# A hybrid HGRN2 + mLSTM layer on one core: finished token tiles are evacuated behind the next weight split, and the steps from w_out to the FFN stand in another order

## The chip, the core and the metric

The kernel runs on one core of a Trainium2 chip. The time is that of one execution on the device, in microseconds (us). A core has a matrix engine (TensorE, PE in the profile; PEld are its weight loads), a vector engine (VectorE, DVE), an activation engine (ScalarE, ACT), a general engine (GpSimd, POOL) and an engine that here only issues transfers (SyncE, SP). Each engine runs its own instructions in the order in which they were issued and waits for others through semaphores. Matrix products are added up in PSUM, from where DVE or ACT must fetch ("evacuate") them.

## The reference

One layer works on 128 context tokens and 256 sample tokens of width D = 2048. Shift, scale and gate come from the conditioning vector. Cut to what matters here, with `rms_norm(x, g) = x * rsqrt(mean(x*x) + EPS) * g`:

```python
h = rms_norm(x, g_pre_mix) * (1.0 + sc_a) + sh_a
y, new_st = mixer(h, ...)        # h @ w_in, HGRN2 and mLSTM scans, w_up, gates, then @ w_out
x = x + gt_a * rms_norm(y, g_post_mix)
h = rms_norm(x, g_pre_ffn) * (1.0 + sc_f) + sh_f
a, b = jnp.split(h @ w_ffn_in, 2, axis=-1)          # D_FF = 5632 each
x = x + gt_f * rms_norm((jax.nn.silu(a) * b) @ w_ffn_out, g_post_ffn)
```

The outputs are x for both groups of tokens and the final scan states of the context tokens.

## The kernel before

All weight matrices are cut into blocks of 128 x 128 and streamed from HBM in the order of use, 16 blocks to a load (`raw`, 3 buffers) and 8 blocks to a *piece*. Products of 32-bit numbers are made of three products of shorter ones: a piece is split by ACT into a high half (`high`, L951, tile `wh`, instruction at L362) and by DVE into the rest (`low`, L962, tile `wl`, L966). Both have 3 buffers; five pieces around the change have buffers of their own (`xwh`, `xwl`). The activations are split in the same way. For each block TensorE then runs high x high, high x low and low x high.

`run_piece` (L1018) is the step of the main loop: it issues the load two units ahead, the `low` of piece i+1, some extra work, the `high` of piece i+2, and then the products of piece i. For most matrices `products` keeps the weights as the stationary operand and 384 tokens as columns (L984 to L986). For w_out and w_ffn_out `products_t` (L994) keeps 128 tokens as the stationary operand and 512 output columns of the weights as the moving one (L1009 to L1011): 18 matmuls to a piece, 6 for each of three token tiles t. A *block end* is the place where the three accumulators of 512 output columns n are finished; `products_t` then calls `evac_t` (L1079) at once.

- For w_out, `evac_out` (L1341) squares the accumulator on ACT (L1315), multiplies it on DVE by the post-norm gain into `yg` (L1344), squares that on ACT and multiplies it by `x1` on DVE with a running sum (L1346). There are 4 blocks of 8 pieces. Of the last block the last 6 pieces are run token by token: token 0 of all six, then token 1, then token 2.
- After a token's last column `norms` (L1353) makes both norm factors from the sums. `x1_part(t, n)` (L1363) forms the new x in 512 columns (DVE, L1365) and its normed copy in `yg` (ACT, L362). `h2_transpose` (L1370) turns four squares of `yg` on TensorE (L1373), and `h2_part` (L1375) applies scale and shift on ACT (L364, tile `h`) and splits into `hi` (DVE, L1383) and `lo` (L1384), the moving operand of the FFN.
- The first three FFN pieces (the head) need only column quarter n = 0. They are run on tokens 0 and 1 first (256 columns), then on token 2 (128 columns). The pieces after them need quarter 1, and so on; each of the next six pieces carries the transposes of one more token tile.
- For w_ffn_out the inner dimension is cut into six groups. Each adds its part to `yacc` in SBUF (L1087). In the last group, `end_tile` (L1506) follows: ACT squares `yacc` (L1315), DVE multiplies by the post-norm gain (L1513); at the last 512 columns it makes the norm factor, adds x in four instructions (L1521) and stores. The last 3 pieces are again run token by token.

The order of all this is that of the program text from w_out on; the planner `schedule` places only the work of the scans and of the late modulation.

## Time and profile before

| | |
|---|---|
| median of 3 runs | 2432.37 us (2429.99 to 2435.18) |
| profiled execution, its own time | 2430.1 us |
| span of its instructions | 2428.3 us |
| PE busy | 2359.6 us (97%) |
| PEld busy | 2210.5 us (91%) |
| DVE busy | 1466.4 us (60%) |
| ACT busy | 931.0 us (38%) |
| mean granted clock | 0.988 |

Busy time is the sum of an engine's instructions; matmuls overlap in the pipeline, so PE's is no measure of its speed. A granted clock of 1.00 is 2.4 GHz, 0.50 is 1.2 GHz. In a list of waits a row names the engine and instruction that waited, behind `<-` the engine and instruction that released it, and then the total, the number of waits and the longest, in us. In a timeline the first number is the start from the beginning of the span, the second the duration; a bracket at the end is the idle time of the engine just before and what ended it. w_out runs from about 1129 to 1275 us, the last group of w_ffn_out from about 2350 us to the end.

### The profile page before, as it was taken

How to read it: one execution, taken by the hardware profiler on the slowest of the kernel's cores; microseconds unless marked ns; L12 is line 12 of the kernel's file. 1: busy time of each engine (PE TensorE's matmuls, PEld its weight loads, DVE VectorE, ACT ScalarE, POOL GpSimd, SP SyncE). 2: the span in 40 equal slices, each digit the busy share in tenths (PEclk: the TensorE clock that was granted, in tenths of full speed). 3: DMA queues.
4: the chain of work that ended last, by engine and by line, in shares of the span. 5: the costliest groups of instructions: out<-in, count | busy, mean ns of one | idle time of the engine just before them, and what ended most of it. 6: DMA issues, size and time to landing. Idle time of an engine off the chain costs nothing. (4 is left out here: it accounts for less than half of the span.)

```text
span 2428.3 us, 33115 instructions
## 1 busy us (share of the span) xinstructions
PE 2359.6 (97%) x13519; PEld 2210.5 (91%) x13519; DVE 1466.4 (60%) x2237; ACT 931.0 (38%) x1384; POOL 207.8 (9%) x277
## 2 busy tenths in 40 slices
PE   7999899999999999999998999999999999999996
PEld 5889899999999999999778998999899899899895
DVE  5777788776657889885344788333333433433435
ACT  5335555655444222224445333332233223223232
POOL 1115743420000000000000000000000000000000
PEclk9999999999999999999998999999999999999998
DMA  8863324333325666665322555333333333333341
GB/s 353 310 251 146 111 101 182 151 131 142 121 79 188 244 230 233 235 226 209 120 104 74 213 219 223 122 122 139 121 123 139 117 126 122 125 134 128 117 174 70
DMA packets 70809, 393.05 MB, mean 162 GB/s; under 512 B 8416, under 2 KB 8576, under 8 KB 36736
## 3 DMA queue, kind: packets, MB, share of 16 engines
q1 hardware_dynamic: 68256, 383.54, 42.3%
q0 software_dynamic: 2400, 7.38, 0.9%
q8 instruction: 106, 1.74, 0.3%
q14 instruction: 47, 0.39, 0.0%
HBM read 386.14 MB, written 4.76 MB: 161 GB/s over the span
## 5 line engine op out<-in xcount | busy, mean ns | idle before, releaser
L984 PE MATMUL mm<-hi,wh 128*128 128x384 f32 (+1 forms) x2944 | 998.4, 339 | 5.6 <-ACT wh L362 3.0
L986 PE MATMUL mm<-hi,wl 128*128 128x384 f32 (+1 forms) x2944 | 985.6, 335 | 0.7 <-DVE wl L966 0.7
L985 PE MATMUL mm<-lo,wh 128*128 128x384 f32 (+1 forms) x2944 | 985.0, 335 | 0.0
L362 ACT ACTIVATE wh<-raw 128x1024 fp32r<-128x1024 f32 x515 | 543.0, 1055 | 628.4 <-PE mm L985 355.7
L966 DVE TENSOR_TENSOR wl<-raw,wh 128x1024 fp32r<-128x1024 f32 x515 | 625.4, 1230 | 168.2 <-ACT wh L362 167.9
L984 PEld LDWEIGHTS mm<-hi,wh 128*128 128x128 f32 x2944 | 555.3, 189 | 17.4 <-issue 8.3
L985 PEld LDWEIGHTS mm<-lo,wh 128*128 128x128 f32 x2944 | 555.1, 189 | 1.4
L986 PEld LDWEIGHTS mm<-hi,wl 128*128 128x128 f32 x2944 | 554.7, 188 | 1.2 <-DVE wl L966 1.2
L820 DVE SCALAR_TENSOR_TENSOR acc_acc<-raw_w,st,acc_acc 128x512 f32<-128x512 f32 x480 | 335.0, 754 | 0.0
L1011 PE MATMUL mm<-wl,gh 128*128 128x512 f32 x528 | 210.7, 399 | 8.6 <-DVE wl L966 8.6
L1009 PE MATMUL mm<-wh,gh 128*128 128x512 f32 x528 | 210.8, 399 | 0.0
L1010 PE MATMUL mm<-wh,gl 128*128 128x512 f32 x528 | 210.2, 398 | 0.0
L1069 DVE TENSOR_TENSOR fs<-mm,fs 128x384 f32<-128x384 f32 x44 | 24.5, 558 | 185.5 <-ACT fs L364 185.5
L1011 PEld LDWEIGHTS mm<-wl,gh 128*128 128x128 f32 x528 | 100.2, 190 | 34.1 <-DVE wl L966 9.9
L1074 DVE TENSOR_TENSOR fs<-mm,fs 128x384 f32<-128x384 f32 x44 | 24.5, 557 | 171.5 <-PE mm L986 171.5
L1009 PEld LDWEIGHTS mm<-wh,gh 128*128 128x128 f32 x528 | 100.1, 190 | 24.2 <-issue 0.4
L1010 PEld LDWEIGHTS mm<-wh,gl 128*128 128x128 f32 x528 | 100.2, 190 | 23.9
L1333 POOL DMA_DIRECT2D d_f<-gt_f x1 | 0.5, 518 | 1202.4 <-ACT gt_f L362 1202.4
L1087 DVE TENSOR_TENSOR yacc<-mm,yacc 128x512 f32<-128x512 f32 x60 | 41.4, 691 | 97.9 <-PE mm L1011 97.6
L362 ACT ACTIVATE gh<-fs 128x384 fp32r<-128x384 f32 x44 | 23.1, 525 | 166.3 <-DVE fs L1074 166.3
L984 PE MATMUL mm<-oh,wh 128*128 128x384 f32 x256 | 86.6, 338 | 0.0
L986 PE MATMUL mm<-oh,wl 128*128 128x384 f32 x256 | 85.9, 336 | 0.0
(307 smaller groups left out, 2072.9 us busy)
## 6 DMA issues: line engine op xcount, KB each, us to landing
raw<-ws SPq DMA_DIRECT2D x260, 1024.0 KB, 5.1
raw_w<-wm SPq DMA_DIRECT2D x128, 512.0 KB, 3.3
wm<-wm SPq DMA_DIRECT2D x64, 512.0 KB, 6.2
xs<-xt SPq DMA_DIRECT2D x4, 768.0 KB, 7.5
x<-xk SPq DMA_DIRECT2D x3, 1024.0 KB, 6.8
out_y<-yacc SPq DMA_DIRECT2D x12, 256.0 KB, 2.1
GM<-d_m POOLq DMA_DIRECT2D x2, 1024.0 KB, 11.5
gain<-d_f POOLq DMA_DIRECT2D x8, 256.0 KB, 5.4
```

The lines of the kernel that those rows point to most:

```text
L362: sc.activation(out, in_, func, bias=0.0, scale=scale)
L820: ve.scalar_tensor_tensor(get(acc)[:, c], get(w)[:, i], col, get(acc)[:, c], ALU.mult, ALU.add)
L966: ve.tensor_tensor(lo, src, hi.bitcast(F32), ALU.subtract)
L984: te.matmul(acc, hi[:, s], xh[:, b:e], start=first, stop=False)
L985: te.matmul(acc, hi[:, s], xl[:, b:e], start=False, stop=False)
L986: te.matmul(acc, lo[:, s], xh[:, b:e], start=False, stop=last)
L1009: te.matmul(acc, xh[:, c], hi[:, s], start=first, stop=False)
L1010: te.matmul(acc, xl[:, c], hi[:, s], start=False, stop=False)
L1011: te.matmul(acc, xh[:, c], lo[:, s], start=False, stop=last)
L1069: ve.tensor_tensor(s, acc, s, ALU.mult)
L1074: ve.tensor_tensor(s, acc, s, ALU.mult)
L1087: ve.tensor_tensor(y, acc, y, ALU.add)
```

## The change

`products_t` no longer evacuates a finished accumulator at once: it puts the evacuation on a list `post`, and `flush` issues the list. `run_piece` calls `flush` behind the `low` of the next piece and ahead of everything else. In the last group the products with the post-norm gain go on the same list, so that they come behind the three adds. Where pieces are written out by hand, `flush` is called behind the splits. The sum with `x1` in `evac_out` writes a spare SBUF tile (one of the two buffers of `h`) and no longer the accumulator. Transposes and `h2_part` of a tile become one step `part_u`, issued ahead of the products that it stood beside; the `x1_part` steps and the `high` and `low` of four FFN pieces move, and no computation is added or left out.

```diff
@@ -1011,7 +1011,14 @@
                 te.matmul(acc, xh[:, c], lo[:, s], start=False, stop=last)
                 seen[k] += 1
                 if last:
-                    evac_t(key, t, accs.pop(k))
+                    post.append(lambda key=key, t=t, acc=accs.pop(k): evac_t(key, t, acc))
+
+    post = []
+
+    def flush():
+
+        while post:
+            post.pop(0)()
 
     pos = [0]
 
@@ -1020,6 +1027,7 @@
         if i % 2 == 0:
             load(i // 2 + RAW - 1)
         low(i + 1)
+        flush()
         for o in placed.get(i, ()):
             o.fn()
         for fn in extra:
@@ -1343,7 +1351,8 @@
         square(junk, acc, stats[:, t, 0, n:n + 1])
         ve.tensor_tensor(y, acc, GM[:, CT[t], col(n)], ALU.mult)
         square(junk, y, stats[:, t, 1, n:n + 1])
-        ve.scalar_tensor_tensor(acc, y, 2.0, x1[:, t, col(n)], ALU.mult, ALU.mult,
+        junk2 = fp.tile([P, 512], F32, tag="h2", bufs=2, name="h2")
+        ve.scalar_tensor_tensor(junk2, y, 2.0, x1[:, t, col(n)], ALU.mult, ALU.mult,
                                 accum_out=stats[:, t, 2, n:n + 1])
 
     def x_square(k):
@@ -1407,13 +1416,18 @@
         run_piece(todo)
 
 
+
+    def part_u(t, n):
+        h2_transpose(t, n)
+        h2_part(t, n)
+
     run_piece()
     run_piece([lambda: load((a0 + 4) // 2), lambda: high(a0 + 2)])
-    last = [a0 + k for k in range(TAIL_OUT)]
-    pos[0] = p_ffn
-    high(a0 + 3)
     low(a0 + 1)
     low(a0 + 2)
+    flush()
+    last = [a0 + k for k in range(TAIL_OUT)]
+    high(a0 + 3)
     load(p_ffn // 2)
     high(a0 + 4)
     low(a0 + 3)
@@ -1423,32 +1437,32 @@
     load(p_ffn // 2 + 1)
     for i in last:
         products_t(i, (0,), True)
+    flush()
     norms(0)
     x1_part(0, 0)
+    high(p_ffn)
     x1_part(0, 1)
-    high(p_ffn)
     low(p_ffn)
     load(p_ffn // 2 + 2)
     for i in last:
         if i == last[-1]:
-            h2_transpose(0, 0)
+            part_u(0, 0)
         products_t(i, (1,), True)
+    flush()
     norms(1)
-    h2_part(0, 0)
     x1_part(1, 0)
     for k, i in enumerate(last):
         if i == last[-1]:
-            h2_transpose(1, 0)
+            high(p_ffn + 2)
+            low(p_ffn + 2)
+            part_u(1, 0)
         products_t(i, (2,), False)
-        if k == 1:
+        if k == 0:
             high(p_ffn + 1)
             low(p_ffn + 1)
-        if k == 2:
-            high(p_ffn + 2)
-            low(p_ffn + 2)
     load(p_ffn // 2 + 3)
+    flush()
     norms(2)
-    h2_part(1, 0)
     x1_part(2, 0)
 
 
@@ -1457,35 +1471,28 @@
     cur.clear()
     cur.update(h2)
     head = [p_ffn + k for k in range(HEAD_FFN)]
+    x1_part(1, 1)
     for i in head:
         if i == head[-1]:
-            h2_transpose(2, 0)
+            part_u(2, 0)
         products(i, (0, 2 * P), True)
-    h2_part(2, 0)
     for k, i in enumerate(head):
-        x1_part(k, 1) if k else None
-        if k == 1:
-            h2_transpose(0, 1)
-            h2_part(0, 1)
-        if k == 2:
-            h2_transpose(1, 1)
-            h2_part(1, 1)
-        products(i, (2 * P, T))
+        part_u(k, 1)
         if k == 0:
+            x1_part(2, 1)
             high(p_ffn + 3)
             low(p_ffn + 3)
         if k == 1:
+            x1_part(0, 2)
             high(p_ffn + 4)
-    h2_transpose(2, 1)
-    h2_part(2, 1)
+        products(i, (2 * P, T))
     pos[0] = p_ffn + HEAD_FFN
 
     rest = [(t, n) for n in (2, 3) for t in range(3)]
-    x1_part(*rest[0])
     for k, (t, n) in enumerate(rest):
-        todo = [lambda t=t, n=n: h2_transpose(t, n), lambda t=t, n=n: h2_part(t, n)]
+        todo = [lambda t=t, n=n: part_u(t, n)]
         if k + 1 < len(rest):
-            todo.insert(0, lambda r=rest[k + 1]: x1_part(*r))
+            todo.append(lambda r=rest[k + 1]: x1_part(*r))
         run_piece(todo)
     close_pool("f")
     close_pool("wx")
@@ -1510,16 +1517,16 @@
         y = yacc[0][:, t, col(n)]
         square(junk2[3], y, ysum[:, t, n:n + 1])
         if n < 3:
-            ve.tensor_tensor(y, y, GF[n][:, CT[t]], ALU.mult)
+            post.append(lambda: ve.tensor_tensor(y, y, GF[n][:, CT[t]], ALU.mult))
             return
...
@@ -1536,13 +1543,14 @@
         cur.update(gts if pieces[i][0][3][0] == "fo" else h2)
         run_piece(todo)
     last = [n_pieces - TAIL_FO + k for k in range(TAIL_FO)]
-    pos[0] = n_pieces
     for i in last:
         high(i)
         low(i)
+    flush()
     for t in range(3):
         for i in last:
             products_t(i, (t,), True)
+        flush()
     for name in list(pools)[::-1]:
         close_pool(name)
```

DVE at the first block end in w_out (`wl`: low half of a piece; L1344/L1352 the product with the gain, L1346/L1355 the sum), before:

```order
```order
L1318 TENSOR_TENSOR acol<-acol,vt 128x32
L966 TENSOR_TENSOR wl<-raw,wh 128x1024 x8
L1344 TENSOR_TENSOR yg<-mm,GM 128x512
L1346 SCALAR_TENSOR_TENSOR mm,stats<-yg,x_11124 128x512
L1344 TENSOR_TENSOR yg<-mm,GM 128x512
L1346 SCALAR_TENSOR_TENSOR mm,stats<-yg,x_11124 128x512
L1344 TENSOR_TENSOR yg<-mm,GM 128x512
L1346 SCALAR_TENSOR_TENSOR mm,stats<-yg,x_11124 128x512
L966 TENSOR_TENSOR wl<-raw,wh 128x1024 x8
```

and now:

```order
```order
L1326 TENSOR_TENSOR acol<-acol,vt 128x32
L966 TENSOR_TENSOR wl<-raw,wh 128x1024 x9
L1352 TENSOR_TENSOR yg<-mm,GM 128x512
L1355 SCALAR_TENSOR_TENSOR h_11351,stats<-yg,x_11124 128x512
L1352 TENSOR_TENSOR yg<-mm,GM 128x512
L1355 SCALAR_TENSOR_TENSOR h_11356,stats<-yg,x_11124 128x512
L1352 TENSOR_TENSOR yg<-mm,GM 128x512
L1355 SCALAR_TENSOR_TENSOR h_11361,stats<-yg,x_11124 128x512
L966 TENSOR_TENSOR wl<-raw,wh 128x1024 x8
```

One more split stands ahead of the three token tiles. ACT at the head of the FFN (`h`: scaled and shifted transposes; `yg`: normed x; `wh`, `xwh`: high half of a piece), before, from the end of `norms(2)`:

```order
```order
L364 ACTIVATE tot<-tot,zero 128x1
L364 ACTIVATE h_12016<-tp,mod_110,acol 128x128 x4
L362 ACTIVATE yg<-x_11124,tot 128x512
L364 ACTIVATE h_12108<-tp,mod_110,acol 128x128 x4
L362 ACTIVATE wh<-raw 128x1024
L362 ACTIVATE yg<-x_11124,tot 128x512
L364 ACTIVATE h_12150<-tp,mod_110,acol 128x128 x4
L362 ACTIVATE xwh<-raw 128x1024
L362 ACTIVATE yg<-x_11124,tot 128x512
L364 ACTIVATE h_12191<-tp,mod_110,acol 128x128 x4
L364 ACTIVATE h_12227<-tp,mod_110,acol 128x128 x4
L362 ACTIVATE yg<-x_11124,tot 128x512 x2
```

and now, from the same place:

```order
```order
L364 ACTIVATE tot<-tot,zero 128x1
L362 ACTIVATE yg<-x_11124,tot 128x512 x2
L364 ACTIVATE h_12098<-tp,mod_110,acol 128x128 x4
L364 ACTIVATE h_12134<-tp,mod_110,acol 128x128 x4
L362 ACTIVATE yg<-x_11124,tot 128x512
L362 ACTIVATE wh<-raw 128x1024
L364 ACTIVATE h_12176<-tp,mod_110,acol 128x128 x4
L362 ACTIVATE yg<-x_11124,tot 128x512
L362 ACTIVATE xwh<-raw 128x1024
L364 ACTIVATE h_12217<-tp,mod_110,acol 128x128 x4
L364 ACTIVATE h_12254<-tp,mod_110,acol 128x128 x4
L362 ACTIVATE yg<-x_11124,tot 128x512
```

Before, the first `h` here is that of token 1; it now stands further up, ahead of token 2's squares and norm factors. Each `yg` (the product of an `x1_part`) now follows the `h` of the tile before it, where it stood ahead of it. DVE at the end of the last group (L1087/L1095 the adds, L1513/L1520 the gain products, `tail` the last 512 columns), before:

```order
```order
L966 TENSOR_TENSOR wl<-raw,wh 128x1024 x3
L1087 TENSOR_TENSOR yacc<-mm,yacc 128x512
L1513 TENSOR_TENSOR yacc<-yacc,gain 128x512
L1087 TENSOR_TENSOR yacc<-mm,yacc 128x512
L1513 TENSOR_TENSOR yacc<-yacc,gain 128x512
L1087 TENSOR_TENSOR yacc<-mm,yacc 128x512
L1513 TENSOR_TENSOR yacc<-yacc,gain 128x512
L966 TENSOR_TENSOR wl<-raw,wh 128x1024 x2
L1087 TENSOR_TENSOR yacc<-mm,yacc 128x512
L1515 TENSOR_TENSOR tail<-yacc,gain 128x512
```

and now:

```order
```order
L966 TENSOR_TENSOR wl<-raw,wh 128x1024 x3
L1095 TENSOR_TENSOR yacc<-mm,yacc 128x512 x3
L1520 TENSOR_TENSOR yacc<-yacc,gain 128x512 x3
L966 TENSOR_TENSOR wl<-raw,wh 128x1024 x4
L1095 TENSOR_TENSOR yacc<-mm,yacc 128x512 x3
L1520 TENSOR_TENSOR yacc<-yacc,gain 128x512 x3
L1095 TENSOR_TENSOR yacc<-mm,yacc 128x512
L1522 TENSOR_TENSOR tail<-yacc,gain 128x512
L1524 TENSOR_REDUCE tot<-ysum 128x1
```

The last two splits stand ahead of the third block's evacuation where they stood behind it, and its gain products follow the three adds.

## Rows read from the trace of the kernel before

**Rows 1.** Waits of PE, 1060:1350 and 2340:2430: total, times, longest
```profile
PE mm L1011 <- DVE wl L966: 7.1, 3, 2.4
PE mm L984 <- DVE hi L1383: 6.6, 1, 6.6
PE tp L1373 <- ACT yg L362: 6.3, 2, 4.3
...
PE mm L1011 <- DVE wl L966: 8.6, 3, 4.8
```

**Rows 2.** PE timeline, first and third w_out wait: start, duration
```profile
1168.92 0.50 PE L1011 MATMUL mm<-wl,hi 128*128 128x512 f32 x1 [2.40 <-DVE wl L966]
...
1241.16 0.50 PE L1011 MATMUL mm<-wl,hi 128*128 128x512 f32 x1 [2.34 <-DVE wl L966]
```

**Rows 3.** Windows: length, busy time by engine, PEclk, DMA, GB/s
```profile
1210.00:1230.00 20.00, 20.00 (x90) 16.57 (x89) 6.13 (x5) 4.90 (x5) 0.00 (x0) 1.00 0.36 124
1205.30:1208.50 3.20, 3.20 (x9) 2.44 (x9) 1.22 (x2) 0.00 (x0) 0.00 (x0) 0.51 0.89 333
...
2389.80:2393.00 3.20, 3.20 (x9) 2.52 (x8) 0.98 (x1) 0.00 (x0) 0.00 (x0) 0.52 0.00 0
```

**Rows 4.** ACT and DVE timeline, splits after the three blocks
```profile
1168.59 1.04 ACT L362 ACTIVATE wh<-raw 128x1024 fp32r<-128x1024 f32 x1
...
1203.09 1.99 ACT L362 ACTIVATE wh<-raw 128x1024 fp32r<-128x1024 f32 x2
...
1239.99 1.04 ACT L362 ACTIVATE wh<-raw 128x1024 fp32r<-128x1024 f32 x1
...
1239.88 1.22 DVE L966 TENSOR_TENSOR wl<-raw,wh 128x1024 fp32r<-128x1024 f32 x1
```

**Rows 5.** PE timeline, token 1 of the last block, and transposes (L1373)
```profile
1254.72 0.39 PE L1009 MATMUL mm<-wh,hi 128*128 128x512 f32 x1
...
1290.23 0.60 PE L1373 MATMUL tp<-ct,yg 128*128 128x128 f32 x4
...
1296.24 0.62 PE L1373 MATMUL tp<-ct,yg 128*128 128x128 f32 x4
...
1299.33 0.62 PE L1373 MATMUL tp<-ct,yg 128*128 128x128 f32 x4
...
1327.38 0.60 PE L1373 MATMUL tp<-ct,yg 128*128 128x128 f32 x4
...
1331.98 0.60 PE L1373 MATMUL tp<-ct,yg 128*128 128x128 f32 x4
```

**Rows 6.** Timeline, token 0 of the last block; two groups by line
```profile
1254.98 0.69 ACT L1315 ACTIVATE junk<-mm,zero 128x512 f32<-128x512 f32 x1 [7.02 <-PE mm L1011]
...
1255.80 0.69 DVE L1344 TENSOR_TENSOR yg<-mm,GM 128x512 f32<-128x512 f32 x1 [6.39 <-ACT junk L1315]
...
1259.77 1.34 ACT L362 ACTIVATE yg<-x,tot 128x512 f32<-128x512 f32 x2
...
L1365 DVE SCALAR_TENSOR_TENSOR x<-yg,tot,x 128x512 f32<-128x512 f32 x12 | 8.9, 745 | 0.0
L1346 DVE SCALAR_TENSOR_TENSOR mm<-yg,x 128x512 f32<-128x512 f32 x12 | 8.4, 700 | 0.4
```

**Rows 7.** ACT and DVE timeline, one unit in the order h, lo, yg
```profile
1279.84 1.49 ACT L364 ACTIVATE h<-tp,mod,acol 128x128 f32<-128x128 f32 x4
...
1281.82 0.69 DVE L1384 TENSOR_TENSOR lo<-h,hi 128x512 fp32r<-128x512 f32 x1
...
1283.27 0.72 ACT L362 ACTIVATE yg<-x,tot 128x512 f32<-128x512 f32 x1 [1.94 <-DVE x L1365]
```

**Rows 8.** DVE timeline, the end of the last group
```profile
2396.93 0.69 DVE L1087 TENSOR_TENSOR yacc<-mm,yacc 128x512 f32<-128x512 f32 x1 [6.15 <-PE mm L1011]
...
2409.59 0.69 DVE L1087 TENSOR_TENSOR yacc<-mm,yacc 128x512 f32<-128x512 f32 x1 [3.59 <-PE mm L1011]
...
2419.80 0.68 DVE L1087 TENSOR_TENSOR yacc<-mm,yacc 128x512 f32<-128x512 f32 x1
```

More of the change, by code (lines that the diff above doesn't have):

```diff
@@ L1518, in end_tile @@
         rstd1(r, s, D)
-        for n in (3, 0, 1, 2):
-            y, o = yacc[0][:, t, col(n)], junk2[t] if n == 3 else yacc[0][:, t, col(n)]
-            ve.scalar_tensor_tensor(y, o, r, x1[:, t, col(n)], ALU.mult, ALU.add)
-            sy.dma_start(out_y[:, t, col(n)], y)
+        for m in (3, 0, 1, 2):
+            y, o = yacc[0][:, t, col(m)], junk2[t] if m == 3 else yacc[0][:, t, col(m)]
+            ve.scalar_tensor_tensor(y, o, r, x1[:, t, col(m)], ALU.mult, ALU.add)
+            sy.dma_start(out_y[:, t, col(m)], y)
     last_fb = last_piece["fb", KF - 1]
```

## The prediction

> **What bounds the kernel now.** I read the page first: TensorE is busy 97% of the 2428.3 us span and no other engine passes 60%, so time is won only where TensorE stands still, or where work follows its last matmul. Next I read its list of waits, cut to the two stretches that the change touches [rows 1]: w_out and the start of the FFN, and the last FFN output group. The reader is to see few, long waits: 20.0 us in the first stretch, 8.6 in the second. Third, the timeline of TensorE at those waits [rows 2, 5]: in w_out it waits each time for a `wl`, the low half of the weight split, in the second piece after a block of 512 output columns is finished. Fourth, what DVE and ACT do then [rows 4, 6]: DVE is still multiplying, squaring and adding the three finished token tiles, and the `wl` stands behind that in its queue. Last, the granted clock [rows 3]: after the second w_out wait it is 0.51 for 3.2 us, so TensorE is near 1.2 GHz instead of 2.4; the same follows other waits.
>
> A matmul of 512 columns takes (20 + 0.39)/90 = 0.227 us from start to start at full clock [rows 3], so a piece of 18 takes 4.08, and one token's 6 of a piece 1.36.
>
> **A. The three block ends in w_out.** Now the split of piece i+1 stands ahead of the evacuation of piece i-1. The first wait is 2.40 us idle after a matmul of 0.39, 2.79 from start to start, so 2.56 lost; the third loses 2.51 [rows 2]. What is late next: the `wh` behind the squares on ACT, and its `wl`. At the first end that `wh` starts at 1168.59 [rows 4], takes 1.04, and its `wl` 1.22 more, so that is there at 1170.9. TensorE wants it 18 matmuls after 1168.92 - 2.56, at 1170.4: 0.5 is waited, 2.1 won. At the other two no square of `x` stands before the `wh`, which comes 0.7 earlier: nothing is waited. These win 2.56 and 2.51, and 1.6 each for the stretch at half clock that then has no cause (half of 3.2). At the third the split must also feed six pieces at token pace: `wh` at 1239.99 gives `wl` by 1242.3, then one every 1.2 against 1.36 wanted. **A = 2.1 + 4.2 + 4.1 = 10.4.** The squared product with `x1` now writes a spare SBUF tile instead of PSUM: 12 instructions of 0.70, and the nearest row that goes from SBUF to SBUF is 0.745 [rows 6]. On the path it stands three times, so between 0.7 x 3 = 2.1 worse and 2.1 better; I take the near row, 0.1, as nothing.
>
> **B. From w_out into the FFN.** Before, from the square of token 0 at 1254.98 [rows 6] to the last transposes at 1331.98 [rows 5] pass 77.0 us. TensorE's own work in it: two tokens of 8.16 and transposes of 0.36 (17.0); three pieces of 256 columns and three of 128 with four transposes (6.01 from 1290.23 to 1296.24 is one of each and a transpose, 3.09 to 1299.33 is a small piece with its transpose, so 2.92, 2.71 and 0.38: 18.4); five units of 4.60 (1327.38 to 1331.98); less 0.26 by which the square starts after token 1's first matmul, 1254.72: 58.2. So 18.8 is lost now, 12.9 of it in the waits [rows 1], the rest at half clock.
>
> After, I follow the queues as printed. The parts: square to `yg` is 4.79, of which 3.97 from the product with GM [rows 6]; `h` to the end of `lo` is 1281.82 + 0.69 - 1279.84 = 2.67 and `h` to `yg` 3.43 [rows 7], in just the order h, hi, lo, x1, yg that now stands everywhere; a `wh` holds ACT for 0.95 (two take 1.99 [rows 4]).
> - Let token 1 be finished at time 0. The `h` of token 0 ends at 0.35 and its `lo` holds DVE to 1.57; then the product, `yg` at 5.54, two `wh` as before, and `h` of token 1 at 8.04, now ahead of token 2's squares and norm factors where it stood behind them; its `lo` is ready at 10.7. TensorE comes to the first FFN piece at 8.16 + 0.36 = 8.5: 2.1 waited, where 6.6 was.
> - Count now from 8.5. Token 2: square 0.9, product 2.1, `yg` 6.1; its transposes are due at 7.9, no wait. `h`, hi and lo are done at 11.2, when the 128-column pieces want them.
> - Those pieces go at 3.09 each, but x1_part now stands behind part_u in both queues, so that a unit runs h, hi, lo, x1, yg, wh in one chain: 3.43 + 0.62 + 0.95 = 5.0 (0.62 is what a `yg` holds ACT for, 1.34 for two less 0.72). Three units from 11.2: TensorE is at the first 384-column piece at 20.9, the `lo` of (2,1) at 24.5: 3.7 waited, where 4.3 was and the half clock behind it.
> - The last five units want 4.60 and get 5.0; the first has slack, the others wait 0.3 to 0.4, 1.4 in all.
>
> 2.1 + 3.7 + 1.4 = 7.2. Two of the waits are of the length after which the clock fell before; each such stretch costs up to 1.6, none costs nothing, and of 3.2 for both I take 2.2. **B = 18.8 - 7.2 - 2.2 = 9.4**, with 7.2 to 11.6 from the clock alone.
>
> **C. The last FFN group.** Two block ends: 8.6 - 4.8 = 3.8 idle [rows 1], plus 0.16 each as above, 4.1, and one stretch at half clock (0.52 for 3.2 us [rows 3]): 5.7. All go, since ACT's squares no longer wait for a gain product on DVE between the adds; the next `wh` comes sooner too. Then the end. Before, the first add of the third block is at 2396.93 and the last piece's first add at 2409.59, with three chains of 5.1 (10.21 from 2409.59 to 2419.80) and 8.5 to the end [rows 8]. After, the `wl` of the last piece comes first: its `wh` can start when the block's last piece leaves the buffer, some 1.2 after 2396.93 (the 6 matmuls of the two other tokens, less 0.26), so `wl` is done at +3.4; three adds and three gains of 0.69, the gains behind their squares, bring it to +7.2 with a little overlap. So the chains begin 12.66 - 7.2 = 5.5 sooner. TensorE's wait of 4.8 and its half clock go as well, but that is worth no more: DVE's three chains of 5.1 are longer than the three tokens of 4.2 that TensorE needs, and set the end. **C = 5.7 + 5.5 = 11.2.**
>
> **At nothing:** the deferred adds of the other FFN groups (TensorE waits for none of them now, and DVE has 40% free; without that cover each block would wait for a split of 1.22), the loads (the same order on SP; each is let go by a `wl`, which now comes earlier), and POOL.
>
> **Sum:** 10.4 + 9.4 + 11.2 = 31.0. The profiled execution's own time is 2430.1 (1.8 around its span), so 2399.1; the median of the three runs is 2.3 higher, which gives 2401.4. I say **2400 us**.
>
> **Rivals.**
> 1. The FFN start only moves its waits. For it: x1_part is behind part_u, and two `wh` still stand ahead of an `h`. If every slip of the chain adds to the next and the clock stays low through the small pieces, B is about 0: 2430.1 - 21.6 = 2408.5, with the median's 2.3 up to 2411. Against it: the counted queues. 0.15.
> 2. No wait is left, because `yg` and `h` come a little sooner than I chain them: B = 18.8 and A half a us more: 2389 to 2392. For it: several margins in B are under 0.5. Against it: the unit of 5.0 is a sum of durations that hardly vary. 0.10.
> 3. The tail keeps its start: if the gains are held back, the 5.5 of C is lost: 2404.5 to 2407. Against it: all three adds are ready when DVE reaches them. 0.10.
> 4. Slower: deferral holds the accumulators longer. Six banks serve blocks of three. If the next block but one, or the first FFN accumulators, came to a bank whose add still stood behind the split, TensorE would wait for a split and an add, 1.22 + 0.69 = 1.9, at each of 24 FFN block ends: 46 - 31, so 2445. It decides once DVE is more than a block late, 3 pieces of 4.2 in the last group. Against it: no wait for an accumulator is among the listed waits [rows 1], and the split that is put ahead can run a whole piece earlier, so the evacuation still starts when its matmuls end. 0.03. Beside this: the Trainium skill, page "PSUM — Partial Sum Buffer", section "Summary: rules for kernel authors", says to evacuate promptly, PSUM being tight; by that rule deferral costs, by the rows there is room, and the sum goes by the rows.
>
> **How the numbers follow.** Forecast 0.62 (2394 to 2406 with the clock's bounds and the spare tile's 2.1), rivals 0.15, 0.10, 0.10 and 0.03. Reaching into rivals 1 to 3 gives 2392 to 2410 for 8 in 10. Differences under 0.2% (5 us) can't be told from no change here. Faster needs only A or C to be half right; the rest of rival 1 and the case of both A and C gone give 0.03 for the same, rival 4 gives 0.03 for slower: 0.94 for faster.
>
> **What would show it.** Right: no wait of TensorE for a `wl` over 0.6 us in w_out or the last group; a wait near 2 us for `hi` or `lo` at the first FFN piece and one near 3.7 at the first 384-column piece; then units of 5.0; three end chains of 5.1 that begin some 7 us after the third block's first finished token. Wrong: waits for PSUM tiles, a longer first FFN wait than 6.6, or end chains that start where they did.

## The result and the profile after

The changed kernel takes 2400.63 us (median of 4 runs, 2397.82 to 2402.32) where the kernel before takes 2431.6 (4 runs beside it): a ratio of 0.9869, 95% interval 0.9852 to 0.9887. Forecast were 2400 us and a range of 2392 to 2410. The profiled execution took 2399.97 us with a span of 2398.2; before it was 2430.1 with 2428.3.

The waits of TensorE from w_out to the end, in the changed kernel (who waits <- whom it waits for: total, times, longest):

```profile
PE mm L984 <- DVE hi L1392: 3.2, 2, 2.1
PE mm L1011 <- DVE wl L966: 0.4, 1, 0.4
PE mm L985 <- DVE lo L1393: 0.3, 1, 0.3
PE tp L1382 <- ACT yg L362: 0.3, 1, 0.3
```

Before, these were 20.0 us in the first stretch and 8.6 in the last group [rows 1]; now 4.2 are left in all, and the last group has none. The waits for `wl` are down to one of 0.36, at the first block end in w_out, where 0.5 was worked out. TensorE's timeline of the changed kernel (start, duration; the bracket is the idle time just before and what ended it) shows what stands where:

```profile
1130.74 0.40 PE L1009 MATMUL mm<-wh,hi 128*128 128x512 f32 x1
...
1172.95 0.50 PE L1011 MATMUL mm<-wl,hi 128*128 128x512 f32 x1 [0.36 <-DVE wl L966]
...
1246.36 0.39 PE L1009 MATMUL mm<-wh,hi 128*128 128x512 f32 x1
...
1264.89 0.38 PE L984 MATMUL mm<-hi,xwh 128*128 128x256 f32 x1 [1.09 <-DVE hi L1392]
...
1287.23 0.69 PE L984 MATMUL mm<-hi,wh 128*128 128x384 f32 x1 [2.15 <-DVE hi L1392]
...
1293.31 0.60 PE L1382 MATMUL tp<-ct,yg 128*128 128x128 f32 x4
...
1298.18 0.66 PE L1382 MATMUL tp<-ct,yg 128*128 128x128 f32 x4
...
2335.61 0.39 PE L1009 MATMUL mm<-wh,gh 128*128 128x512 f32 x1
```

The rows are the first matmul of w_out, the wait for `wl`, token 1's first matmul in the last block, the first FFN piece, the first 384-column piece, two transposes of the six units behind it, and the first matmul of the last group. Token 1's first matmul is the moment at which token 0 is finished [rows 5]. A unit, from transpose to transpose, takes 4.87 or 4.95, where 4.60 was read before [rows 5].

At the end of the last group, DVE's timeline of the changed kernel answers to [rows 8]:

```profile
2374.47 1.23 DVE L966 TENSOR_TENSOR wl<-raw,wh 128x1024 fp32r<-128x1024 f32 x1 [2.97 <-ACT wh L362]
2375.61 1.88 DVE L1095 TENSOR_TENSOR yacc<-mm,yacc 128x512 f32<-128x512 f32 x3
2377.41 1.31 DVE L1520 TENSOR_TENSOR yacc<-yacc,gain 128x512 f32<-128x512 f32 x2
...
2379.48 0.68 DVE L1095 TENSOR_TENSOR yacc<-mm,yacc 128x512 f32<-128x512 f32 x1
...
2384.61 0.68 DVE L1095 TENSOR_TENSOR yacc<-mm,yacc 128x512 f32<-128x512 f32 x1
...
2389.68 0.68 DVE L1095 TENSOR_TENSOR yacc<-mm,yacc 128x512 f32<-128x512 f32 x1
```

The split of the last piece (2374.47) stands ahead of the three adds of the third block, the gain products behind them, and the three end chains begin at 2379.48, 2384.61 and 2389.68, 5.1 apart as before. The last piece of the third block starts at 2369.21; before it started at 2393.93 and the first add came 3.0 later, so token 0 is finished at 2372.2 now. The first chain begins 7.3 after that, where 12.66 was.

Differences of starts on TensorE give four stretches that can be compared between kernels, whatever happens ahead of w_out (us):

| kernel | first w_out matmul to token 0 finished | from there to the last transposes | first matmul of the last group to that of its last three pieces | from there to the end |
|---|---|---|---|---|
| before | 125.97 | 77.26 | 43.70 | 30.17 |
| changed | 115.62 | 66.66 | 37.80 | 24.79 |
| won | 10.35 | 10.60 | 5.90 | 5.38 |

That is 32.2. Between the last transposes and the last group 1022.59 us pass now and 1022.45 before, no difference. Ahead of w_out, which the change doesn't touch, the changed kernel's profile happens to be 2.0 longer (w_out begins at 1130.74, before at 1128.75). 32.2 - 2.0 - 0.1 = 30.1, the difference of the two profiled executions. Over the fourteen profiles of this study that start lies between 1128.0 and 1132.7, while the stretches of unedited code agree within 0.1 (the second one, with its stretch at half clock, within 1.5: 66.59 to 68.08): so effects of 1 to 3 us are read below from the stretches, and only larger ones from the medians.

### The profile page after: what moved, and what is told of

It reads as the page before. It is cut to its first block, busy times and chain, and to the rows that moved or that the text cites. A ratio compares the mean times of both kernels' runs of the same rounds, so it can differ in the third digit from the quotient of the medians.

```text
span 2398.2 us, 33132 instructions
## 1 busy us (share of the span) xinstructions
PE 2350.6 (98%) x13519; PEld 2203.4 (92%) x13519; DVE 1469.8 (61%) x2237; ACT 930.5 (39%) x1384; POOL 207.6 (9%) x277
## 4 chain that ended last, share of the span: by engine, by line
PE 89%; DVE 4%; POOL 3%; ACT 3%; issue 1%; DVEq 0%; POOLq 0%; ACTq 0%
PE mm L984 21%; PE mm L986 21%; PE mm L985 21%; PE mm L1011 7%; PE mm L1009 7%; PE mm L1010 7%; PE mv L1143 1%; POOL cb L418 1%; DVE wl L966 1%; POOL pp L586 1%; PE o_o L733 1%; ACT h L364 0%; ACT wh L362 0%; PE sc_pa L828 0%; POOL pp L589 0%
## 5 line engine op out<-in xcount | busy, mean ns | idle before, releaser
L966 DVE TENSOR_TENSOR wl<-raw,wh 128x1024 fp32r<-128x1024 f32 x515 | 627.5, 1230 | 259.4 <-ACT wh L362 259.1
L362 ACT ACTIVATE wh<-raw 128x1024 fp32r<-128x1024 f32 x515 | 543.1, 1055 | 626.1 <-PE mm L985 353.8
L362 ACT ACTIVATE gh<-fs 128x384 fp32r<-128x384 f32 x44 | 23.1, 525 | 166.3 <-DVE fs L1082 166.3
L985 PE MATMUL mm<-o,wh 128*128 128x384 f32 x256 | 85.6, 335 | 0.0
## 6 DMA issues: line engine op xcount, KB each, us to landing
GM<-d_m POOLq DMA_DIRECT2D x2, 1024.0 KB, 11.3
```

The lines of the kernel that those rows point to most:

```text
L362: sc.activation(out, in_, func, bias=0.0, scale=scale)
L966: ve.tensor_tensor(lo, src, hi.bitcast(F32), ALU.subtract)
L985: te.matmul(acc, hi[:, s], xl[:, b:e], start=False, stop=False)
```

## The experiments

All are edits of the changed kernel. None leaves computation out. Their stretches and times:

| kernel | w_out to token 0 | to last transposes | last group | end | median us | ratio to before, 95% |
|---|---|---|---|---|---|---|
| changed | 115.62 | 66.66 | 37.80 | 24.79 | 2400.63 | 0.9869 (0.9852 to 0.9887) |
| 1 w_out at once | 127.57 | 66.99 | 37.79 | 24.79 | 2411.93 | 0.9913 (0.9898 to 0.9928) |
| 2 w_ffn_out at once | 115.63 | 68.08 | 43.71 | 30.22 | 2414.21 | 0.9919 (0.9902 to 0.9936) |
| 3 old order at the FFN | 115.67 | 75.75 | 37.80 | 24.77 | 2410.84 | 0.9909 (0.9894 to 0.9923) |
| 4 gains between the adds | 115.61 | 66.97 | 37.79 | 27.60 | 2401.22 | 0.9871 (0.9857 to 0.9886) |
| 5 last splits behind the adds | 115.67 | 68.06 | 37.80 | 26.95 | 2400.37 | 0.9872 (0.9857 to 0.9886) |
| 6 sum back in PSUM | 115.63 | 66.59 | 37.80 | 24.75 | 2399.39 | 0.9867 (0.9853 to 0.9880) |
| 7 adds held a block | 115.61 | 66.95 | 37.80 | 24.76 | 2400.51 | 0.9874 (0.9860 to 0.9889) |
| 8 x1 first in the units | 115.66 | 65.74 | 37.79 | 24.82 | 2400.47 | 0.9872 (0.9858 to 0.9886) |
| 9 x1 early at the head | 115.60 | 62.22 | 37.80 | 24.76 | 2396.86 | 0.9855 (0.9841 to 0.9869) |
| 10 both, and POOL at the end | 115.67 | 61.80 | 37.79 | 25.24 | 2396.52 | 0.9852 (0.9838 to 0.9866) |
| 11 high half ahead of x1 | 115.66 | 62.05 | 37.80 | 23.46 | 2394.06 | 0.9844 (0.9830 to 0.9858) |
| 12 x1 two tiles ahead | 115.64 | 60.26 | 37.79 | 23.47 | 2390.21 | 0.9827 (0.9814 to 0.9841) |

**1. w_out evacuated at once.**

```diff
-                    post.append(lambda key=key, t=t, acc=accs.pop(k): evac_t(key, t, acc))
+                    if key[0] == "out":
+                        evac_t(key, t, accs.pop(k))
+                    else:
+                        post.append(lambda key=key, t=t, acc=accs.pop(k): evac_t(key, t, acc))
```

> The changed kernel, but a finished accumulator of w_out is evacuated at once again; w_ffn_out stays deferred and the order at the FFN start stays new. Theory (each wait is a matter of its own queue): the three waits of TensorE for a low half behind the evacuation come back, 2.4 us each, with half clock behind two of them; from the first w_out matmul to the finished token 0 it takes 126.0 us instead of the 115.6 of the changed kernel, the rest stays: 2400.6 + 10.4 = 2411.0. Rival (the terms are not additive): what w_out loses gives DVE and ACT time to catch up, the waits at the FFN start shrink, and under 5 us are lost: 2401 to 2405.

The first stretch grew by 11.95, to 127.57, and no other changed; the time rose by 11.3. Theory: the head absorbs nothing. The expected 126.0 was the old kernel's; the 1.6 above it is a third stretch at half clock. TensorE waited three times for `wl` as before (7.2 us, longest 2.4), the first time just as long as before the change; behind it the full clock was granted in the kernel before, and half in this one. The rows are windows of 3.2 us: length, busy time of PE, PEld, DVE, ACT and POOL, granted clock, DMA share, GB/s; first the kernel before, then this one:

```profile
1169.00:1172.20 3.20, 3.20 (x14) 2.65 (x15) 2.10 (x2) 3.00 (x6) 0.00 (x0) 1.00 0.64 246
```

```profile
1172.40:1175.60 3.20, 3.20 (x8) 2.52 (x9) 2.10 (x2) 3.00 (x6) 0.00 (x0) 0.50 0.67 215
```

**2. w_ffn_out added at once, gains between the adds.**

```diff
-                    post.append(lambda key=key, t=t, acc=accs.pop(k): evac_t(key, t, acc))
+                    if key[0] == "fo":
+                        evac_t(key, t, accs.pop(k))
+                    else:
+                        post.append(lambda key=key, t=t, acc=accs.pop(k): evac_t(key, t, acc))
...
-            post.append(lambda: ve.tensor_tensor(y, y, GF[n][:, CT[t]], ALU.mult))
+            ve.tensor_tensor(y, y, GF[n][:, CT[t]], ALU.mult)
```

> The changed kernel, but finished accumulators of w_ffn_out are added at once and the products with the post-norm gain stand between the adds, as before the change. Theory: two waits of 1.9 with a stretch at half clock come back (43.7 us instead of 37.8 from the first matmul of the last group to token 1 of its last three pieces) and the three end chains begin 12.7 instead of 7.3 after the first add of the third block, 5.4 later: 2400.6 + 11.3 = 2411.9. Rival: the end is set by TensorE, not by the DVE chains, so only the 5.9 of the block ends come back: 2406.5.

(The row read is the first matmul of the last three pieces, which is token 0's; "token 1" there is a slip.) The third stretch is 43.71, the fourth 30.22: both as before the change, 5.91 and 5.43 back. TensorE's wait for `wl` is back as well:

```profile
PE mm L1011 <- DVE wl L966: 9.0, 4, 4.8
```

That is the old 8.6 of the last group and the 0.4 of w_out. The rival's sum, 5.9 alone, is out: the fourth stretch lost its 5.4 too. Whether TensorE or DVE sets the end isn't shown by this, since TensorE's wait of 4.8 came back in the same stretch and the first end chain waits for TensorE here, as before [rows 8]; experiment 4 parts the two. The median rose by 13.6. 1.4 of that lies at the FFN start, which the edit doesn't touch: half clock lasted longer behind the wait at the first 384-column piece. The second 3.2 us behind that wait (windows), in the changed kernel and in this one:

```profile
1290.50:1293.70 3.20, 3.20 (x22) 3.17 (x20) 1.46 (x2) 1.67 (x2) 0.00 (x0) 0.98 0.03 5
```

```profile
1292.10:1295.30 3.20, 3.20 (x12) 3.20 (x11) 1.46 (x2) 1.67 (x2) 0.00 (x0) 0.50 0.03 5
```

**3. The old order between the norm factors and the sixth unit, with both deferrals.** The edit puts the kernel before's lines back from `norms(0)` to the loop over `rest`, with `flush()` ahead of `norms(1)` and `norms(2)`.

> The changed kernel with the old written-out order from the norm factors of token 0 to the sixth FFN unit; both deferrals stay. Theory: the 10.6 us of this stretch come back alone (77.3 instead of 66.7 us from the finished token 0 to the last transposes, with waits of 2.0, 6.6 and 4.3): 2411.2. Rival: part of that gain came from the deferral, which lets the squares and sums of the last block run earlier; then the first FFN wait is well under 6.6 and about half comes back: 2406.

75.75 instead of 66.66: 9.1 came back and 10.2 in the median. Its waits are those of before [rows 1]:

```profile
PE mm L984 <- DVE hi L1392: 6.9, 1, 6.9
PE tp L1382 <- ACT yg L362: 6.3, 2, 4.3
...
```

The rival had expected well under 6.6 for the first of them. That 1.5 less came back than expected is the clock: the waits are as long, but over this stretch (a window of each, first before the change) the mean granted clock is 0.89 there and 0.93 here, and the same matmuls keep TensorE busy for 64.19 and 62.42.

```profile
1254.72:1331.98 77.26, 64.19 (x381) 59.47 (x380) 37.23 (x64) 42.01 (x90) 0.00 (x0) 0.89 0.15 55
```

```profile
1248.33:1324.08 75.75, 62.42 (x382) 58.07 (x380) 36.82 (x64) 41.75 (x90) 0.00 (x0) 0.93 0.19 71
```

The two deferrals and the order are thus separate gains: undone one at a time they cost 11.95, 11.3 and 9.1 in their own stretches.

**4. The gain products between the deferred adds.**

```diff
-            post.append(lambda: ve.tensor_tensor(y, y, GF[n][:, CT[t]], ALU.mult))
+            ve.tensor_tensor(y, y, GF[n][:, CT[t]], ALU.mult)
```

> The changed kernel, but the products with the post-norm gain stand between the three deferred adds instead of behind them. Theory: then ACT's square of a token waits for the gain product of the token before, the next high half stands behind three squares and comes 2.7 us later (a block takes 6.7 on DVE as before the change, against 4.0). In the changed kernel the low half behind it is ready at 2352.5 and TensorE wants it at 2352.9, so about 2.2 are waited at two block ends, with or without 1.6 of half clock each, and the end chains begin 2.7 later: 7.1 to 10.3, 2408 to 2411. Rival: putting the adds behind the split is the whole effect and the order of the gains is worth nothing: 2400.6.

Half of the theory fell. The third stretch is 37.79, unchanged, and TensorE waits nowhere in the last group. DVE's timelines, one line of the changed kernel and then this one:

```profile
2351.23 1.23 DVE L966 TENSOR_TENSOR wl<-raw,wh 128x1024 fp32r<-128x1024 f32 x1 [0.26 <-ACT wh L362]
```

```profile
2342.81 1.23 DVE L966 TENSOR_TENSOR wl<-raw,wh 128x1024 fp32r<-128x1024 f32 x1 [2.96 <-ACT wh L362]
2344.70 0.69 DVE L1095 TENSOR_TENSOR yacc<-mm,yacc 128x512 f32<-128x512 f32 x1 [0.67 <-PE mm L1011]
2346.28 0.69 DVE L1520 TENSOR_TENSOR yacc<-yacc,gain 128x512 f32<-128x512 f32 x1 [0.88 <-ACT tail L1323]
2346.89 0.68 DVE L1095 TENSOR_TENSOR yacc<-mm,yacc 128x512 f32<-128x512 f32 x1
...
2350.75 0.69 DVE L1520 TENSOR_TENSOR yacc<-yacc,gain 128x512 f32<-128x512 f32 x1 [0.94 <-ACT tail L1323]
2351.70 2.36 DVE L966 TENSOR_TENSOR wl<-raw,wh 128x1024 fp32r<-128x1024 f32 x2 [0.26 <-ACT wh L362]
...
2379.95 0.68 DVE L1095 TENSOR_TENSOR yacc<-mm,yacc 128x512 f32<-128x512 f32 x1
```

A block does take 6.7 (2344.70 to 2351.44), and the split behind it is 2.8 later: 18.39 us after the group's first matmul (2333.31 here), where it was 2351.23 - 2335.61 = 15.62. But I had taken the `wl` for the one of the next piece; that one had been put ahead of the adds. The `wl` behind them is for the piece after it, a whole piece (4.2 us) later. Only at the end, where no piece follows, did the 2.8 show: the chains begin at 2379.95, 46.64 after the group's first matmul instead of 43.87, and the fourth stretch is 27.60 instead of 24.79 (the median, 0.6 higher, doesn't show it). This also answers the rival of experiment 2: TensorE's last matmul starts 50.16 us after the group's first one, 50.17 in the changed kernel, and the end is 2.8 later all the same. In the changed kernel DVE sets the end.

**5. The last two splits behind the third block's evacuation.**

```diff
+    flush()
     for i in last:
         high(i)
         low(i)
-    flush()
```

> The changed kernel, but in front of the last three pieces the evacuation of the third block (three adds, then three gain products) stands ahead of the last two low halves, as it did before the change; the gains still follow the adds. With the kernel that has the gains between the adds it parts the 5.4 us that the end won. Theory (count of DVE's queue): adds from 2372.2 in the changed kernel's time, gains to 2376.3, the two splits to 2377.5 and 2378.7; TensorE wants the first at 2375.2, waits 2.3 and finishes token 0 at 2380.1, so the end chains begin 8.3 after the first finished token instead of 7.3, or 9.9 if the clock falls: 1.0 to 2.6 more, 2401.6 to 2403.2. Rival: with the gains behind the adds the place of the splits doesn't matter, 2400.6.

2.16 in the fourth stretch, with one wait of 1.98 for `wl` and half clock behind it: the theory, between its two figures. The median didn't show it (2400.37): 2 us is less than its runs differ. So of the 5.4 that the end won, undoing the gains behind the adds takes back 2.8 and undoing the splits ahead 2.2; the remaining 0.4 belongs to neither alone.

**6. The sum with x1 back in the accumulator.**

```diff
-        junk2 = fp.tile([P, 512], F32, tag="h2", bufs=2, name="h2")
-        ve.scalar_tensor_tensor(junk2, y, 2.0, x1[:, t, col(n)], ALU.mult, ALU.mult,
+        ve.scalar_tensor_tensor(acc, y, 2.0, x1[:, t, col(n)], ALU.mult, ALU.mult,
```

> The changed kernel, but the running sum with x1 in w_out writes back into the accumulator, as before the change, and not into a spare tile. Theory: the instruction takes 0.69 to 0.70 either way and nothing waits for the bank, so 0 (115.6 us from the first w_out matmul to the finished token 0): 2400.6. Rival: the spare tile cost or won up to 0.7 for each of three tokens on the path, 2.1 to either side: 2398.5 or 2402.7.

Nothing moved (115.63, 66.59). The instruction took 700 ns into the accumulator and 692 into the spare tile.

**7. Adds held back a whole block** (the rival "slower" of the prediction).

```diff
-                    post.append(lambda key=key, t=t, acc=accs.pop(k): evac_t(key, t, acc))
+                    fn = lambda key=key, t=t, acc=accs.pop(k): evac_t(key, t, acc)
+                    if key[0] == "fo" and key[1] < n_groups - 1:
+                        held.append((i + 1 + (4 if key[1] < 4 else 3), fn))
+                    else:
+                        post.append(fn)
...
+        while held and held[0][0] <= pos[0]:
+            held.pop(0)[1]()
```

> The changed kernel, but the adds of the first five groups of w_ffn_out are held back to the last place that the six accumulators allow: just ahead of the first matmul that needs the bank again, one block later. It tries the rival of the prediction that deferral holds accumulators too long. By that rival TensorE waits for a split and an add, 1.9 us or, if the split ends 2.35 after a piece begins and one add follows, 3.0, at 15 block ends (three in each of five groups): 28 to 45 more, up to 24 more if the clock falls each time: 2429 to 2470. By the opposite theory, which the kernel with the gain products between the adds speaks for (its later splits made TensorE wait nowhere), the queues of DVE run a whole piece ahead of TensorE there and the adds are done in time: 2400.6.

TensorE has no wait behind the FFN start, and the time is 2400.51. The edit holds the adds of the first five groups. (In the first group they are copies on ACT.) The first adds of the second group, in the changed kernel and in this one (DVE timelines):

```profile
1666.38 2.09 DVE L1095 TENSOR_TENSOR yacc<-mm,yacc 128x512 f32<-128x512 f32 x3 [0.72 <-PE mm L1011]
```

```profile
1681.20 1.88 DVE L1103 TENSOR_TENSOR yacc<-mm,yacc 128x512 f32<-128x512 f32 x3
```

Counted from the first w_out matmul (1130.74 and 1129.32) they come 16.2 us later, of the 16.8 that a block of four pieces takes, and TensorE still finds the bank free: DVE's queue is far enough ahead of it. So in these five groups the rival is not only absent, its price is nil even at the limit; the last group was not held. The page "PSUM — Partial Sum Buffer" of the Trainium skill, section "Summary: rules for kernel authors", says to evacuate promptly. With six banks for blocks of three this kernel's time doesn't depend on it there, up to a whole block.

**8. x1 ahead of the transposed tile, in the six units.**

```diff
-            todo.append(lambda r=rest[k + 1]: x1_part(*r))
+            todo.insert(0, lambda r=rest[k + 1]: x1_part(*r))
```

> The changed kernel, but in the six units behind the FFN head the step that forms the next tile of x stands ahead of the transposed tile's scale, shift and split, as before the change. Theory: a unit is now one chain through both queues (4.95 from transpose to transpose in the changed kernel); with the step ahead the normed copy is ready when TensorE comes and a unit falls to TensorE's own 4.60. Four or five units win 0.35 each, 1.5 us: 2399.1. The wait of 2.2 at the first 384-column piece stays. Rival: the unit is held by the reuse of the two transpose banks or of the two h tiles, so it stays at 4.95: 2400.6.

From one unit's transposes to the next it takes 4.60, 4.60, 5.07 and 4.60: 0.9 won, not 1.5. ACT's normed copies in two successive units of this kernel:

```profile
1291.27 0.72 ACT L362 ACTIVATE yg<-x,tot 128x512 f32<-128x512 f32 x1 [3.02 <-DVE x L1374]
...
1296.40 0.72 ACT L362 ACTIVATE yg<-x,tot 128x512 f32<-128x512 f32 x1 [2.07 <-DVE x L1374]
```

They are 5.13 apart. The loop is only another one: x1 now waits behind the split on DVE, and its normed copy stands ahead of the scaled tile on ACT. TensorE lived on its lead for two units and lost 0.47 in the third. The theory (TensorE's own 4.60) had followed one queue and not the loop through both.

**9. x1 early at the FFN head.**

```diff
     x1_part(1, 1)
+    x1_part(2, 1)
...
         if k == 0:
-            x1_part(2, 1)
+            x1_part(0, 2)
             high(p_ffn + 3)
             low(p_ffn + 3)
-        if k == 1:
-            x1_part(0, 2)
+        if k == 2:
             high(p_ffn + 4)
```

> The changed kernel, but x of token 2 in the second column quarter and x of token 0 in the third are formed earlier (the first in a gap of ACT ahead of the first scaled tile, the second behind the second scaled tile), and one high half of a split is issued behind the last scaled tile of the quarter. Theory: the wait of 2.2 at the first 384-column piece is the chain scale, hi, lo, next x, normed copy, high half, scale run three times in a row; without the x steps in it the last tile is split some 0.3 after TensorE wants it. The wait, the 0.6 at the transposes and the stretch at half clock behind it, 4.7 in all, go: 2396. Rival: it is held by the transposes themselves (TensorE issues them between the 128-column pieces), and under 1 us is won: 2400.

66.66 became 62.22, 4.4 won; the median 3.8 less. TensorE's waits from w_out on:

```profile
PE mm L984 <- DVE hi L1392: 1.1, 1, 1.1
PE mm L1011 <- DVE wl L966: 0.4, 1, 0.4
PE mm L985 <- DVE lo L1393: 0.3, 1, 0.3
```

The 2.15 at the first 384-column piece and the half clock behind it are gone. So the wait that the change left there was the chain of scaled tile, split, x1 and high half, as the prediction had it. The edit takes two x1 steps and one high half out of that chain together; which of them suffices was not tried.

**10. Both steps of 8 and 9, one split moved, and the end helped by POOL.** To the edits of 8 and 9 come `high` and `low` of the third FFN piece behind `part_u(1, 0)`, and at the end:

```diff
-            ve.scalar_tensor_tensor(y, o, r, x1[:, t, col(m)], ALU.mult, ALU.add)
+            if t < 2 and m != 3:
+                act(y, o, AF.Copy, scale=r)
+                gp.tensor_tensor(y, y, x1[:, t, col(m)], ALU.add)
+            else:
+                ve.scalar_tensor_tensor(y, o, r, x1[:, t, col(m)], ALU.mult, ALU.add)
```

> Both steps of the two kernels beside it, one high and low half moved behind the scaled tile of token 1, and at the end three of the four output quarters of tokens 0 and 1 scaled on ACT and added on POOL instead of DVE. Theory: the units 1.5, the 384-column piece 4.7 and the first FFN wait 0.6 less, 6.8; at the end DVE sheds 6 instructions of 0.69 but ACT's squares come up to 1.7 later, so 2 to 2.6 less: 2400.6 - 9 = 2391 to 2393. Rival at the end: POOL takes longer than the DVE chain or slows DVE beside it, and the end gains nothing or loses up to 3: 2394 to 2397. Rival at the FFN start: half is won, 2394 with the end as in the theory.

FFN start: 4.9 won, of 6.8, the units being short of their part as in 8. The end: 25.24, 0.45 worse. What happened is in the groups of DVE at the end (busy time, mean ns of one), first of the changed kernel, then of this one, and in this kernel's timelines of DVE and POOL:

```profile
L1528 DVE SCALAR_TENSOR_TENSOR yacc<-yacc,tot,x 128x512 f32<-128x512 f32 x9 | 6.2, 743 | 0.0
L1095 DVE TENSOR_TENSOR yacc<-mm,yacc 128x512 f32<-128x512 f32 x6 | 3.9, 682 | 0.0
...
L1522 DVE TENSOR_TENSOR tail<-yacc,gain 128x512 f32<-128x512 f32 x3 | 2.1, 692 | 0.1
```

```profile
L1532 DVE SCALAR_TENSOR_TENSOR yacc<-yacc,tot,x 128x512 f32<-128x512 f32 x3 | 4.1, 1413 | 0.0
L1095 DVE TENSOR_TENSOR yacc<-mm,yacc 128x512 f32<-128x512 f32 x6 | 3.9, 683 | 0.0
L1522 DVE TENSOR_TENSOR tail<-yacc,gain 128x512 f32<-128x512 f32 x3 | 3.1, 1021 | 0.1
```

```profile
2381.75 0.88 DVE L1532 SCALAR_TENSOR_TENSOR yacc<-tail,tot,x 128x512 f32<-128x512 f32 x1 [0.69 <-ACT tot L364]
...
2385.95 4.08 DVE L1532 SCALAR_TENSOR_TENSOR yacc<-yacc,tot,x 128x512 f32<-128x512 f32 x3
```

```profile
2379.07 9.74 POOL L1530 TENSOR_TENSOR yacc<-yacc,x 128x512 f32<-128x512 f32 x6 [45.68 <-issue]
```

DVE shed six instructions. While POOL ran its adds (2379.07 to 2388.8), those of DVE that read two tensors from SBUF were slowed unevenly. The product with the gain took 1.32 and 1.05, where token 0's, ahead of POOL's first add, took 0.69. Of the three in the 4.08 above, two took 1.75 and the third, begun behind POOL's last add, 0.74. `yacc<-tail,tot,x` took 0.88 and 0.75, the second no longer than without POOL. The adds that read an accumulator (`yacc<-mm,yacc`) stayed at 683 ns. The page "GPSIMD Engine Reference" of the Trainium skill, section "1. Specifications", says that the two engines share their way to SBUF and contend when DVE has two inputs from there. The trace agrees for five of the six such instructions that ran beside POOL, with factors of 1.2 to 2.4.

The 0.45 itself lies behind DVE. From the first add of token 0's chain to DVE's last instruction it takes 14.30 us (2375.73 to 2390.03), where it took 15.35: slowed as it is, DVE is done 1.05 sooner. But the span ends 4.9 us after that, where it ended 3.4 after it. SyncE waited 7.1 us for POOL's adds before it issued stores, and for the 2.5 us behind DVE's end the DMA engines are full. That the late stores make the longer end is read from the trace and was not tried apart. So the rival's sum holds: POOL slows DVE, and the end loses.

**11. The high half of the split ahead of x1 in the units, DVE's pauses filled at the end.** To 9 and the moved split of 10 come:

```diff
-        todo = [lambda t=t, n=n: part_u(t, n)]
+        todo = [lambda t=t, n=n: part_u(t, n), lambda: high(pos[0] + 2)]
...
+        if t:
+            out_late.pop(0)()
+        for m in (3, 0, 1) if t < 2 else (3, 0, 1, 2):
+            out(m)
+        if t < 2:
+            out_late.append(lambda: out(2))
```

> For a version faster than the changed kernel: x of token 2 (second quarter) and of token 0 (third quarter) formed early; a high and low half behind the scaled tile of token 1; in the six units the high half of the split ahead of the step that forms the next x; at the end one instruction of tokens 0 and 1 moved into the pause of DVE in the next token's chain. Theory: the loop of a unit loses the 0.95 of the high half, 4.95 - 0.95 = 4.0 is under TensorE's 4.60, so the units win 0.3 each, 1.5; the 384-column piece 4.5 and the first FFN wait 0.4 as measured; 6.4 in all from the finished token 0 to the last transposes (60.3 instead of 66.7 us); the end 1.4 (two pauses of 0.69): 2400.6 - 7.8 = 2392.8. Rival: the loop closes over another engine as it did with the x step in front, the units keep 4.95 and the first waits return: 2394.5 to 2396.

The end won 1.33, as worked out (two pauses of 0.69). The units stayed at 4.88 to 4.93 (the last at 5.19), as the rival had it, but the long waits ahead of them did not return. ACT in one unit of this kernel:

```profile
1291.41 0.72 ACT L362 ACTIVATE yg<-x,tot 128x512 f32<-128x512 f32 x1 [0.94 <-DVE x L1374]
1292.94 1.50 ACT L364 ACTIVATE h<-tp,mod,acol 128x128 f32<-128x128 f32 x4 [0.81 <-PE tp L1382]
1294.32 1.07 ACT L362 ACTIVATE wh<-raw 128x1024 fp32r<-128x1024 f32 x1
1296.33 0.72 ACT L362 ACTIVATE yg<-x,tot 128x512 f32<-128x512 f32 x1 [0.93 <-DVE x L1374]
```

The normed copy waits for x1, TensorE's transposes (at 1292.18) for the copy, and the scaled tile for the transposes: the loop now ran through ACT, DVE and TensorE.

**12. x1 two tiles ahead.** To 11, `x1_part` is cut in its DVE half (`x_new`) and its ACT half (`x_norm`):

```diff
         todo = [lambda t=t, n=n: part_u(t, n)]
         if k + 1 < len(rest):
-            todo.append(lambda r=rest[k + 1]: x1_part(*r))
+            todo.insert(0, lambda r=rest[k + 1]: x_norm(*r))
+        if k + 2 < len(rest):
+            todo.append(lambda r=rest[k + 2]: x_new(*r))
```

> The version before it, but in the six units DVE forms x two tiles ahead and ACT makes the normed copy of the next tile at the unit's start. In the version before, a unit still took 4.91: scale 1.38, hi 0.46, lo 0.60, x 0.67, normed copy 0.66, transposes and their latency 0.87, and scale again; the high half was no longer in that loop but TensorE's transposes were. Theory: x made two tiles ahead opens the loop, a unit falls to TensorE's 4.60, and four to five units win 0.3: from the finished token 0 to the last transposes 60.5 instead of 62.05 us, 2394.1 - 1.5 = 2392.5. Rival: another engine closes the loop again (the two h tiles or transpose banks), units stay at 4.9: 2394.

A unit takes 4.60 (the first 4.65), the second stretch 60.26 (60.5 expected), and the kernel 2390.21 us, 0.9827 (0.9814 to 0.9841) of before: faster than the changed kernel, the intervals being apart. What TensorE still waits for from w_out to the end:

```profile
PE mm L984 <- DVE hi L1399: 0.7, 1, 0.7
PE mm L1011 <- DVE wl L966: 0.4, 1, 0.4
PE mm L985 <- DVE lo L1400: 0.3, 1, 0.3
```

## Why the prediction was right, and where not

| step | predicted | measured |
|---|---|---|
| A, three block ends in w_out | 2.1 + 4.2 + 4.1 = 10.4 | 2.03 + 4.32 + 4.00 = 10.35 |
| B, w_out into the FFN | 9.4 | 10.60 |
| - lost at the first FFN piece | 2.1 | 1.9 |
| - lost at the first 384-column piece, with its transposes | 3.7 | 3.1 |
| - lost in the units | 1.4 | 1.3 |
| - half clock behind the waits | 2.2 | 1.9 |
| C, block ends of the last group | 5.7 | 5.90 |
| C, the end | 5.5 | 5.38 |
| sum | 31.0 | 32.2 |

The measured losses of B are what the gaps between matmul starts have beyond those at full clock; for the units it is four of them, 19.71, less 4 x 4.60. They make 8.2, where 9.4 was forecast and 18.8 was before.

**A is shown.** Undoing that deferral alone brought the three waits back and touched nothing else (1). That the first end keeps a small wait, since `x_square` stands ahead of its `wh`, came out too (0.36 idle, 0.5 worked out).

**B was undersized by 1.2.** Both waits are where they were put, and 0.2 and 0.6 shorter. The half clock was taken at 2.2 for two stretches of up to 1.6; there was one, of 1.9, and it lies behind the second wait. So 1.6 is not the most that a stretch costs: in experiment 2 the one at the same place cost 1.4 more, 3.3. In the seven profiles that leave this stretch's code as it is, it takes 66.59 to 68.08, which makes B 9.2 to 10.7 against the one profile of before: the miss is no larger than what the clock there varies by. The bounds "7.2 to 11.6 from the clock alone" don't follow either: with 0 to 3.2 lost at half clock the sum gives 8.4 to 11.6. The granted clock of the changed kernel behind the first and the second wait:

```profile
1264.90:1268.10 3.20, 2.85 (x21) 2.66 (x22) 2.32 (x6) 1.56 (x6) 0.00 (x0) 1.00 0.74 307
1287.30:1290.50 3.20, 3.16 (x9) 2.76 (x10) 3.17 (x5) 0.81 (x3) 0.00 (x0) 0.50 0.00 0
```

Full (2.4 GHz) behind the first, half (1.2) behind the second. The chain that was named for the second wait is shown by taking x1 and a high half out of it (9): the wait and the half clock behind it went. The unit of 5.0 was right as a number (4.95); that it is a loop whose members can be exchanged without getting shorter (8, 11) wasn't seen.

**C was right in both sums, but one of its reasons was not.** The text says that the waits at the two block ends go "since ACT's squares no longer wait for a gain product on DVE between the adds; the next `wh` comes sooner too". Putting the gains back (4) cost nothing there: the split ahead of the adds does it without that order, since it leaves the next one a whole piece of time. Where the order of the gains does count is the end, 2.8 of its 5.4; the splits ahead give 2.2 (5). That DVE sets the end is shown by 4. The rivals "the tail keeps its start" and "the FFN start only moves its waits" are out by the fourth and second stretch; "slower" by experiment 7. "No wait is left" is out too, with 8.2 still lost in B.

**At nothing:** the spare tile (6) and the deferred adds of the first five groups (7) cost nothing, as costed. Loads were not tried apart.

**Luck.** The medians differ by 30.97, just the 31.0 of the sum, while the stretches won 32.2. In the two profiles a start of w_out that is 2.0 later, with no cause in the change, takes away more than the 1.2 by which B was undersized; how much of that scatter is in the medians isn't known. So the sizes of A and C and the places of B's waits were foreseen, and the agreement to within a microsecond is partly luck.

## What to carry to other kernels

Where an in-order engine both feeds the next step and clears away the last one, put the feed ahead: it buys the feed one whole step of slack, and how the clearing is ordered behind it then hardly matters, until the end, where no step follows. That holds here for a DVE that is busy for 60% of the time, and with room for two blocks in PSUM; a fuller engine was not tried. Here a wait that was a loop through several queues did not get shorter by exchanging its members; what helped was to cut the edge that carries it over to the next turn by working one item further ahead (8 and 11 against 12). Small steps are best measured by stretches between marks on the bounding engine: here the time ahead of the edited part scattered by 4.7 us, more than most single effects.

## What the runs showed of the hardware

- The same wait of TensorE, 2.40 us at the same place, was followed by a granted clock of 1.00 in one kernel and 0.50 in another (experiment 1), and waits of 1.09 and 0.35 by 1.00. So what half clock costs behind a wait of some 2 us differed from run to run: nothing, 1.6 (experiment 1), 1.9 in the changed kernel, 3.3 in experiment 2. What decides it was not found.
- Instructions of DVE with two inputs from SBUF took 1.32, 1.05, 1.75, 1.75 and 0.88 us beside adds of POOL, where 0.69 to 0.75 was usual, and once 0.75; adds with an input from PSUM stayed at 0.68 (experiment 10).
